# Even mixer of a two-block layer: pooled branch with tokens on partitions, its moving means as a matrix product, low parts on GpSimd, norm pivot from five tiles

## The chip, the cores and the metric

One core of one Trainium2 chip. The metric is device time in microseconds (us) of one execution; the kernel before takes 1034.3 us (median of 3 runs, 1033.93 to 1035.69). Engines: PE is TensorE (PEld its weight load), DVE is VectorE, ACT is ScalarE, POOL is GpSimd, SP issues DMAs.

## The reference, cut to what matters

x is 256 tokens by 1024. A first block (three mixers and a feed-forward) and an odd mixer are not touched. The change is inside the even mixer, whose input product has five parts of 1024 columns:

```python
p = einsum("btd,dn->btn", h, w_in)
a_val, a_glu, a_gate, b_val, b_gate = split(p, ...)
u = causal_depthwise_conv(a_val * sigmoid(a_glu), conv_w, conv_b)   # 31 taps
ya = silu(layernorm(u, ln_g, ln_b)) * silu(a_gate)
d = multiscale_pool_diff(b_val)     # per group of 256 channels: mean of the last w tokens, less b_val; w = 2, 4, 8, 16
d = einsum("btgc,gce->btge", d, pool_w) + pool_b                    # 4 groups of 256 x 256
yb = d * pool_scale * silu(b_gate)
out = concat([ya, yb]) @ w_out      # 2048 -> 1024
```

The mean at token t divides by min(t + 1, w).

## The kernel before, in words

**Products.** Each f32 operand is split into a high part (rounded, fp32r) and a low part (the rest), and a product is three matmuls (`mm3`, L493 to L496). Weights come as a stream of 128x1024 chunks: SP loads `raw` (L315), `split_to` (L329) makes `whi` on ACT (L347) and `wlo` (L350) on POOL or DVE. The first letter of a plan entry names the engine of the high part, the second that of the low part. In the even mixer the plan is `"ag"` (low parts on POOL), but the chunks numbered 11, 13, 15, 18 and 21 of the stage have theirs on DVE (`EVEN_LO_V`, L341). There are four buffers each for high and low parts, and chunks are split two ahead.

**The stage.** h is kept with channels on partitions (`hh`, `hl`, eight 128x256 tiles each). Two of the eight u tiles come from `x_group_m` (h stationary, 512 columns wide). Then `EVEN_ORDER` (L154) runs: u tiles 2 and 3 (two chunks each), eight b chunks, u tiles 4 to 7, eight a (`a_gate`) chunks, eight g (`b_gate`) chunks. Each chunk is one `w_tile` (L498): 24 matmuls of 128x256, which leave an output tile with channels on partitions and tokens along the row. Four PSUM banks named `mm` hold these outputs.

**Side work.** `tick` (L369) advances a queue of generators between matmuls. `conv31(k)` (L1506) makes convolution tile k: ACT makes ten of the 31 taps (L1523) and two starting values (L1513, L1514), DVE adds 19 taps (L1527) and the ACT pieces (L1530) in PSUM; ACT copies one half out (L1533) and DVE adds the other (L1534). POOL then sums the tiles into `csum` (L1541, L1543). `ln_early` (L1552) forms a pivot for the layer norm: a matmul with ones over the sum of tiles 0 to 6 (L1555), scaled by ACT into SBUF (L1558), taken from each tile by DVE (L1547), squared on ACT (L1549) and summed on POOL (L1562, L1564). `ln` (L1567) starts after six ticks of the output product: ones matmuls over the sum and tile 7 (L1571, L1572), then the tail of the norm.

**Pooled branch.** ACT copies each b tile to `bv` (L1646). `pools(g)` (L1618) makes moving sums for group g by 1 to 4 doubling additions on POOL (L1626, L1627), then DVE scales and subtracts (L1634 to L1637). After the last g chunk a loop of eight (L1672) does two f32 matmuls with `pool_w` (L1676), the gate on DVE (L1679) and the split into `yT` (ACT L488, DVE L489).

**Output.** Sixteen chunks (L1684): the pooled half first (k 0 to 7), then the convolved half, whose k = 8 needs `ln` done.

The order of the instructions on each engine is made by the tile scheduler from this program, and each engine runs its list in order.

Of the kernel before, what the change touches and what calls it, by code (L numbers as in the profile page):

```python
# [83 lines left out]
def pack_weights(i):  # L84
# [69 lines left out]
EVEN_ORDER = ([("u", 2), ("u", 3)] + [("b", t) for t in range(8)] + [("u", t) for t in range(4, 8)]  # L154
# [65 lines left out]
CON = {}  # L220


def _con_layout():
    o = 0
    for n, w in (("id", 128), ("tri", 128), ("bo", 128), ("va", 32), ("vm", 32), ("rc", 64), ("cm", 128)):
# [8 lines left out]
def consts():  # L234
# [44 lines left out]
POOL_FROM = 9  # L279


def body(tc, x, wst, vec, gains, rows, con, cmpw, poolw, rgw, igw, out, dbg=None):
# [3 lines left out]
    with ExitStack() as ctx:  # L286
# [42 lines left out]
        def split_to(c):  # L329
            while st["split"] <= min(c, nch - 1):  # L330
# [10 lines left out]
                if plan["p"] is PLAN_EVEN and i - plan.setdefault("i0", i) in EVEN_LO_V:  # L341
                    how = "av"
# [83 lines left out]
        SY.dma_start(cm_t, con[:, CON["cm"][0]:])  # L426
# [1124 lines left out]

        def ln_early():  # L1552

            pps = o_ps()
            PE.matmul(pps[:, 0:T], lhsT=ones, rhs=sums["c"], start=True, stop=True)  # L1555
            lnt = act.tile([P, 512], F32, name="lnt", tag="btok")
            sums["p"], sums["q"] = lnt[:, 0:T], lnt[:, T:2 * T]
            A.activation(sums["p"], pps[:, 0:T], AF.Copy, scale=1.0 / 896)  # L1558
# [8 lines left out]
        def ln():  # L1567
# [3 lines left out]
            PE.matmul(mps[:, 0:T], lhsT=ones, rhs=sums["c"], start=True, stop=False)  # L1571
# [4 lines left out]
            de, va = sums["c"], sums["q"]  # L1576
            V.scalar_tensor_tensor(de, mps[:, 0:T], 1.0 / D, sums["p"], op0=OP.mult, op1=OP.subtract)
# [40 lines left out]
        def pools(g):  # L1618
            n = g + 1
            src = bv[:, 2 * g:2 * g + 2]  # L1620
            cur = src
            w = 2 ** n
            for lv in range(n):
                sh = 2 ** lv
                nx = g4()[:, 0:544].rearrange("p (k t) -> p k t", k=2)
                G.memset(nx[:, :, 0:16], 0.0)  # L1626
                G.tensor_tensor(nx[:, :, 16:], cur[:, :, 16:], cur[:, :, 16 - sh:272 - sh], op=OP.add)  # L1627
                cur = nx
                yield
            d = src[:, :, 16:]  # L1630
            rc = con_t[:, CON["rc"][0] + 16 * g:CON["rc"][0] + 16 * g + 16]
            hd = s(32, "hd")
            hv = hd.rearrange("p (k t) -> p k t", k=2)
            V.tensor_tensor(hv, cur[:, :, 16:32], rc[:, None, :].to_broadcast([P, 2, 16]), op=OP.mult)  # L1634
            V.tensor_tensor(hv, hv, d[:, :, 0:16], op=OP.subtract)
            V.scalar_tensor_tensor(d[:, :, 16:], cur[:, :, 32:], 1.0 / w, d[:, :, 16:], op0=OP.mult, op1=OP.subtract)
            V.tensor_copy(d[:, :, 0:16], hv)  # L1637
            yield

        pools_q = deque()  # L1640
        turn = 0
        for kind, t in EVEN_ORDER:
            ps = mm_ps(T)
            w_tile(ps, hh, hl)
            if kind == "b":
                A.activation(bv[:, t, 16:], ps, AF.Copy)  # L1646
                if t % 2:
                    pools_q.append(pools(t // 2))
            elif kind == "u":
# [6 lines left out]
                if t == 7:  # L1656
# [10 lines left out]
        for pg in pools_q:
            for _ in pg:
                pass
        eh = [yt(), yt()]  # L1670
        el = [yt(), yt()]
        for e in range(8):  # L1672
            g = e // 2
            ps = mm_ps(T)
            for k in range(2):
                PE.matmul(ps, lhsT=pwt[:, g * 512 + k * 256 + (e % 2) * P:g * 512 + k * 256 + (e % 2) * P + P],  # L1676
                          rhs=bv[:, 2 * g + k, 16:], start=k == 0, stop=k == 1)
            d = bg[:, e]
# [193 lines left out]
```

## Time and profile before

| | |
|---|---|
| median of 3 runs | 1034.3 us (1033.93 to 1035.69) |
| the profiled execution | 1034.19 us; span of its records 1032.4 us |
| busy: PE, DVE, ACT, POOL | 971.4, 813.3, 637.8, 281.8 us |
| even mixer, from the first `w_tile` to the first output matmul | 704.6 to 842.8 us of the span |

A row of a group names line, engine, operation and tiles (out<-in), then busy us and mean ns. Of a wait, the row says who waited for whom. The granted clock (PEclk) is 1 at 2.4 GHz and 0.5 at 1.2 GHz. Instructions on one engine overlap a little, so the pace is the distance between starts, not the duration of one.

### The profile page before, as it was taken

The numbers are of one execution on the slowest core, as the hardware profiler recorded it, in microseconds if no ns is written. First come the engines' busy times: TensorE is split into PE (matmuls) and PEld (weight loads), VectorE is DVE, ScalarE is ACT, GpSimd is POOL, SyncE is SP. The second block draws the span as 40 slices with busy tenths as digits, with TensorE's granted clock in tenths as the row PEclk, the third lists the DMA queues.
The fourth block names the chain that finished last, engine by engine and source line by source line (L and its number), as shares of the span: only waits on it lengthen the run. The fifth ranks groups of instructions, "written<-read, shape, count | busy, mean of one in ns | idle before, by whom it ended". The sixth has DMA issues, their size and how long they took to land.

```text
span 1032.4 us, 16952 instructions
## 1 busy us (share of the span) xinstructions
PE 971.4 (94%) x6134; PEld 847.3 (82%) x6134; DVE 813.3 (79%) x1637; ACT 637.8 (62%) x1180; POOL 281.8 (27%) x210
## 2 busy tenths in 40 slices
PE   8999999999999889999999999999899789899786
PEld 5878988788776689888789999989899777799675
DVE  6787999989768599856665555676998989888985
ACT  7453588866665556644555454558757647678563
POOL 1133023310225454200000000007757931334340
PEclk9999999999999999999999999999989999999898
DMA  7756232264544544666756565674444634554432
GB/s 278 227 185 171 91 116 83 90 177 143 163 125 147 177 144 150 201 188 208 232 179 189 183 187 187 190 254 146 122 162 143 184 100 143 186 163 124 143 103 81
DMA packets 48867, 166.94 MB, mean 162 GB/s; under 512 B 5584, under 2 KB 8080, under 8 KB 48528
## 3 DMA queue, kind: packets, MB, share of 16 engines
q1 hardware_dynamic: 45936, 157.21, 48.3%
q10 hardware_dynamic: 1728, 6.55, 1.8%
q0 software_dynamic: 1120, 2.10, 1.0%
q8 instruction: 48, 0.79, 0.3%
q14 instruction: 35, 0.29, 0.1%
HBM read 163.71 MB, written 1.61 MB: 160 GB/s over the span
## 4 chain that ended last, share of the span: by engine, by line
PE 60%; DVE 21%; ACT 6%; issue 5%; POOL 4%; DMA 3%; POOLq 0%; SPq 0%; ACTq 0%; DVEq 0%
PE mm L494 15%; PE mm L496 14%; PE mm L495 14%; DVE wlo L350 4%; PE sc L496 3%; PE sc L495 3%; PE sc L494 3%; ACT whi L347 2%; DVE sc L1527 2%; PE tp L950 2%; PE o L1112 2%; POOL g L820 1%; POOL wlo L350 1%; DVE f L1749 1%; DMA g<-acd 1%
## 5 line engine op out<-in xcount | busy, mean ns | idle before, releaser
L347 ACT ACTIVATE whi<-raw 128x1024 fp32r<-128x1024 f32 x261 | 275.1, 1056 | 170.5 <-PE mm L496 82.3
L350 DVE TENSOR_TENSOR wlo<-raw,whi 128x1024 fp32r<-128x1024 f32 x213 | 274.7, 1291 | 122.2 <-ACT whi L347 120.2
L496 PE MATMUL mm<-hh,wlo 128*128 128x256 f32 x800 | 231.8, 291 | 16.5 <-POOL wlo L350 9.5
L494 PE MATMUL mm<-hh,whi 128*128 128x256 f32 x800 | 233.7, 292 | 2.3 <-ACT f L1660 2.3
L350 POOL TENSOR_TENSOR wlo<-raw,whi 128x1024 fp32r<-128x1024 f32 x56 | 140.9, 2533 | 344.8 <-ACT whi L347 289.2
L495 PE MATMUL mm<-hl,whi 128*128 128x256 f32 x800 | 230.8, 289 | 0.0
L496 PEld LDWEIGHTS mm<-hh,wlo 128*128 128x128 f32 x800 | 157.4, 197 | 18.7 <-POOL wlo L350 10.3
L494 PEld LDWEIGHTS mm<-hh,whi 128*128 128x128 f32 x800 | 157.7, 197 | 5.6 <-issue 2.6
L495 PEld LDWEIGHTS mm<-hl,whi 128*128 128x128 f32 x800 | 157.5, 197 | 1.3 <-issue 0.8
L494 PE MATMUL mm<-whi,yT 128*128 128x512 f32 x320 | 128.0, 402 | 2.6 <-ACT f L1533 1.2
L495 PE MATMUL mm<-wlo,yT 128*128 128x512 f32 x320 | 126.1, 394 | 3.8 <-DVE wlo L350 3.8
L496 PE MATMUL mm<-whi,yT 128*128 128x512 f32 x320 | 125.6, 393 | 0.0
L494 PE MATMUL mm<-whi,hh 128*128 128x512 f32 (+2 forms) x240 | 96.4, 402 | 0.7 <-ACT hh L485 0.5
L495 PE MATMUL mm<-wlo,hh 128*128 128x512 f32 (+2 forms) x240 | 93.8, 391 | 0.4 <-DVE wlo L350 0.4
L496 PE MATMUL mm<-whi,hl 128*128 128x512 f32 (+2 forms) x240 | 93.6, 390 | 0.0
L932 POOL TENSOR_TENSOR t<-t,cf 128x256 f32<-128x256 f32 (+1 forms) x48 | 40.5, 846 | 157.5 <-DVE cf L931 52.8
L494 PEld LDWEIGHTS mm<-whi,yT 128*128 128x128 f32 x320 | 60.6, 190 | 16.5 <-DVE f L1817 2.0
L495 PEld LDWEIGHTS mm<-wlo,yT 128*128 128x128 f32 x320 | 60.6, 190 | 15.9 <-DVE wlo L350 4.7
L496 PEld LDWEIGHTS mm<-whi,yT 128*128 128x128 f32 x320 | 60.4, 189 | 12.9
L1527 DVE SCALAR_TENSOR_TENSOR sc<-f,vec_t,sc 128x256 f32<-128x256 f32 x152 | 65.4, 478 | 2.8 <-ACT sc L1514 2.5
L495 PE MATMUL sc<-hl,whi 128*128 128x256 f32 x224 | 63.5, 283 | 0.0
L496 PE MATMUL sc<-hh,wlo 128*128 128x256 f32 x224 | 63.4, 283 | 0.0
(434 smaller groups left out, 1873.7 us busy)
## 6 DMA issues: line engine op xcount, KB each, us to landing
raw<-in_wst SPq DMA_DIRECT2D x286, 512.0 KB, 3.6
g<-acd SPq DMA_DIRECT2D x8, 512.0 KB, 4.4
gain<-in_gains ACTq DMA_DIRECT2D x4, 512.0 KB, 4.4
f<-in_cmpw ACTq DMA_DIRECT2D x1, 1024.0 KB, 6.7
kB<-iqd POOLq DMA_DIRECT2D x4, 256.0 KB, 5.9
f<-acd SPq DMA_DIRECT2D x2, 512.0 KB, 7.0
f<-in_poolw ACTq DMA_DIRECT2D x1, 1024.0 KB, 4.9
f<-in_rgw ACTq DMA_DIRECT2D x1, 768.0 KB, 4.4
```

The lines of the kernel that those rows point to most:

```text
L347: hi = A.activation(h, w, AF.Copy)
L350: lo = (G if how[1] == "g" else V).tensor_tensor(l, w, h.bitcast(F32), op=OP.subtract)
L494: PE.matmul(ps, lhsT=ah, rhs=bh, start=first, stop=False)
L495: PE.matmul(ps, lhsT=ah, rhs=bl, start=False, stop=False)
L496: PE.matmul(ps, lhsT=al, rhs=bh, start=False, stop=last)
L820: G.tensor_tensor(tv, tv, smb[:, None, :].to_broadcast([P, 8, P]), op=OP.add)
L932: G.tensor_tensor(p, p, cf[:, :, None].to_broadcast([P, 2, nk]), op=OP.mult)
L950: PE.transpose(tp[:, c:c + P], p[:, si, kb * P:kb * P + P], ident)
L1112: PE.matmul(O["o"][g * 64:g * 64 + 64, q * 256:q * 256 + 256], lhsT=xt[:, c % nb, vo + g * 64:vo + g * 64 + 64], rhs=O["t", g][:, c], star ...
L1527: V.scalar_tensor_tensor(h, u[:, tap:tap + T], w(tap), h, op0=OP.mult, op1=OP.add)
L1749: V.tensor_tensor_scan(at(xc, k0 + i), A_(i), I_(i), 0.0, op0=OP.mult, op1=OP.add)
```

## The change

1. **b part with tokens on partitions.** The eight b chunks become two `x_group` calls (h stationary, 512 columns): 96 matmuls of 128x512 in place of 192 of 128x256. ACT copies four 128x512 results into `bt`.
2. **Moving means as a matrix.** "mean of the last w, less itself" is a constant 256x256 band matrix per group; its two non-zero pieces (128x144 and 128x128) are loaded once as `pmt` (128x1088, 544 KB on the ACT queue). `pooled(g)`, called after a chunks 1, 3, 5, 7, makes four f32 matmuls and an ACT copy into `dT`. The POOL additions and the four DVE instructions of each group are gone.
3. **Mixing between the g chunks.** `mixed(e)` (two f32 matmuls, DVE gate, split) follows g chunk e + 2; 6 and 7 follow the last.
4. **All low parts of the stage on POOL**: `EVEN_LO_V` is gone.
5. **Pivot from tiles 0 to 4**, formed after convolution tile 5 and kept in PSUM; `csum` has a half for the first five and one for the rest. The norm's first step is an ACT copy and a DVE subtraction.

```diff
-EVEN_ORDER = ([("u", 2), ("u", 3)] + [("b", t) for t in range(8)] + [("u", t) for t in range(4, 8)]
+EVEN_ORDER = ([("u", 2), ("u", 3)] + [("b", t) for t in range(2)] + [("u", t) for t in range(4, 8)]
               + [("a", t) for t in range(8)] + [("g", t) for t in range(8)])
...
+    tt = np.arange(2 * P)
+    pm = []
+    for w in (2, 4, 8, 16):
+        m = ((tt[:, None] <= tt[None, :]) & (tt[:, None] > tt[None, :] - w)) / np.minimum(tt + 1, w)[None, :]
+        m = m - np.eye(2 * P)
+        pm += [m[:P, :144], m[P:, P:]]
+    put("pm", np.concatenate(pm, axis=1))
...
-                if plan["p"] is PLAN_EVEN and i - plan.setdefault("i0", i) in EVEN_LO_V:
-                    how = "av"
...
             elif k == 0:
-                sums["c"] = act.tile([P, 512], F32, name="csum", tag="cbt")[:, 0:T]
+                sums["c"] = act.tile([P, 512], F32, name="csum", tag="cbt")
             elif k == 1:
-                G.tensor_tensor(sums["c"], cva[:, 0], d, op=OP.add)
+                G.tensor_tensor(sums["c"][:, 0:T], cva[:, 0], d, op=OP.add)
             else:
-                G.tensor_tensor(sums["c"], sums["c"], d, op=OP.add)
+                G.tensor_tensor(sums["c"][:, 0:T] if k < PIVOT else sums["c"][:, T:],
+                                sums["c"][:, T:] if k > PIVOT else sums["c"][:, 0:T], d, op=OP.add)
...
+        def ln_pivot():
+
+            pps = tp_ps()
+            PE.matmul(pps[:, 0:T], lhsT=ones, rhs=sums["c"][:, 0:T], start=True, stop=True)
+            sums["p"] = pps[:, T:]
+            A.activation(sums["p"], pps[:, 0:T], AF.Copy, scale=1.0 / (PIVOT * P))
...
-            V.scalar_tensor_tensor(de, mps[:, 0:T], 1.0 / D, sums["p"], op0=OP.mult, op1=OP.subtract)
+            A.activation(de, mps[:, 0:T], AF.Copy, scale=1.0 / D)
+            V.tensor_tensor(de, de, sums["p"], op=OP.subtract)
...
+        pmt = act.tile([P, 4 * PM], F32, name="pmt", tag="yT", bufs=4)
+        A.dma_start(pmt, con[:, CON["pm"][0]:CON["pm"][1]])
+        def pooled(g):
+
+            ps = mm_ps()
+            for j in range(2):
+                for m, (t0, t1) in enumerate(((0, 144), (P, T))):
+                    c = g * PM + m * 144
+                    f = (2 * g + j) * P
+                    PE.matmul(ps[:, j * T + t0:j * T + t1], lhsT=bt[:, m, f:f + P], rhs=pmt[:, c:c + t1 - t0],
+                              start=m == 0, stop=m == 1, skip_group_check=True)
+            A.activation(dT[:, 2 * g:2 * g + 2], ps.rearrange("p (k t) -> p k t", k=2), AF.Copy)
...
+            if kind == "b":
+                ps = x_group(hk, lk, 8, 512)
+                for m in range(2):
+                    A.activation(bt[:, m, t * 512:t * 512 + 512], ps[m], AF.Copy)
+                tick(rate["n"])
+                continue
...
             elif kind == "a":
                 A.activation(ag[:, t], ps, AF.Silu)
+                if t % 2:
+                    pooled(t // 2)
             else:
                 A.activation(bg[:, t], ps, AF.Silu)
+                if t >= 2:
+                    mixed(t - 2)
...
+        for e in (6, 7):
+            mixed(e)
```

How the lists of instructions move, at three places. Lines in rows of the change are those of the changed file, where L350 has become L358, L1527 L1534, L1530 L1537, L489 L497, L1679 L1655, and L1541 and L1543 L1548 and L1550.

POOL, from the stage's first low parts (`wlo`) to the addition of the third convolution tile into `csum`, before:

```order
L350 TENSOR_TENSOR wlo<-raw,whi 128x1024 x9
L1627 TENSOR_TENSOR g_8036<-f_7425 128x2x256
L350 TENSOR_TENSOR wlo<-raw,whi 128x1024 x2
L1626 MEMSET g_8397 128x2x16
L1627 TENSOR_TENSOR g_8309<-f_7425 128x2x256
...
L1627 TENSOR_TENSOR g_8538<-f_7425 128x2x256
L1541 TENSOR_TENSOR csum<-f_7505 128x256
L350 TENSOR_TENSOR wlo<-raw,whi 128x1024 x3
L1543 TENSOR_TENSOR csum<-csum,f_7505 128x256
```

and now:

```order
L358 TENSOR_TENSOR wlo<-raw,whi 128x1024 x15
L1548 TENSOR_TENSOR csum<-f_7504 128x256
L358 TENSOR_TENSOR wlo<-raw,whi 128x1024 x6
L1550 TENSOR_TENSOR csum<-csum,f_7504 128x256
L358 TENSOR_TENSOR wlo<-raw,whi 128x1024 x4
```

The moving sums are gone from between the low parts, and the first addition into `csum` stands behind 15 low parts, where it stood behind 12.

PE, around the pivot's matmul with ones, before (in g chunk 5) and now (in a chunk 6, after the third `pooled`):

```order
L494 MATMUL mm<-hh,whi 128x256
L495 MATMUL mm<-hl,whi 128x256
L496 MATMUL mm<-hh,wlo 128x256
L1555 MATMUL o<-csum,ones 128x256
L494 MATMUL mm<-hh,whi 128x256
```

```order
L1643 MATMUL mm<-pmt,f_7425 128x144
L1643 MATMUL mm<-pmt,f_7425 128x128
L502 MATMUL mm<-hh,whi 128x256
L503 MATMUL mm<-hl,whi 128x256
L504 MATMUL mm<-hh,wlo 128x256
L502 MATMUL mm<-hh,whi 128x256
L1563 MATMUL tp<-csum,ones 128x256
```

It comes seven chunks earlier, and needs the sum of five tiles instead of seven.

DVE, at the first gate of the pooled branch, now (before, the eight of them, L1679, stand together behind the last g chunk):

```order
L1534 SCALAR_TENSOR_TENSOR sc<-f_7423,vec_t,sc 128x256 x4
L1537 TENSOR_TENSOR sc<-sc,t_8857 128x512
L1534 SCALAR_TENSOR_TENSOR sc<-f_7423,vec_t,sc 128x256
L1655 SCALAR_TENSOR_TENSOR f_7508<-mm,vec_t,f_7508 128x256
L1537 TENSOR_TENSOR sc<-sc,t_8608 128x512
L497 SCALAR_TENSOR_TENSOR yT<-f_7508,vec_t,yT 128x256
```

Gate and low part of `yT` now lie among the taps of convolution tiles 6 and 7, in the time of the g chunks.

## Rows read from the trace of the kernel before

**Rows 1.** Windows of the even mixer: length, busy us (and count) per engine, granted clock, DMA.

```profile
core 0: us, PE busy (x) PEld busy (x) DVE busy (x) ACT busy (x) POOL busy (x), PEclk, DMA share, GB/s
704.60:727.60 23.00, 23.00 (x193) 22.94 (x192) 19.12 (x40) 22.63 (x48) 22.43 (x11) 1.00 0.65 206
727.60:750.00 22.40, 18.30 (x142) 18.09 (x142) 22.40 (x37) 14.93 (x30) 15.30 (x10) 0.90 0.39 117
750.00:784.00 34.00, 29.34 (x210) 28.94 (x209) 28.84 (x57) 21.51 (x40) 16.95 (x9) 0.86 0.45 157
784.00:826.00 42.00, 36.12 (x287) 35.71 (x285) 41.93 (x84) 27.61 (x53) 37.89 (x29) 0.96 0.53 163
826.00:842.80 16.80, 13.81 (x79) 11.50 (x79) 16.31 (x31) 8.12 (x18) 8.11 (x8) 1.00 0.33 94
```

**Rows 2.** PE's waits from 700 to 900 us: us in total, times, longest.

```profile
PE mm L496 <- POOL wlo L350: 9.2, 3, 4.1
PE o L1555 <- POOL csum L1543: 3.2, 1, 3.2
...
PE mm L494 <- ACT f L1660: 2.3, 1, 2.3
PE mm L1676 <- DVE f L1679: 1.3, 2, 0.7
```

**Rows 3.** Timeline of PE: start us, us, what, idle before.

```profile
694.75 0.39 PE L494 MATMUL mm<-whi,hh 128*128 128x512 f32 x1
...
697.25 0.39 PE L496 MATMUL mm<-whi,hl 128*128 128x512 f32 x1
697.48 1.03 PE L627 MATMUL sc<-con_t,t 128*128 128x128 f32 x8
...
707.75 0.28 PE L494 MATMUL mm<-hh,whi 128*128 128x256 f32 x1
...
710.62 0.28 PE L494 MATMUL mm<-hh,whi 128*128 128x256 f32 x1
...
767.10 0.41 PE L494 MATMUL mm<-hh,whi 128*128 128x256 f32 x1
767.31 0.41 PE L495 MATMUL mm<-hl,whi 128*128 128x256 f32 x1
```

**Rows 4.** The pooled mixer's matmuls in that timeline.

```profile
831.47 2.75 PE L1676 MATMUL mm<-f,f 128*128 128x256 f32 x12
```

**Rows 5.** Groups by line, 703 to 860 us: busy us, mean ns, idle before.

```profile
L1636 DVE SCALAR_TENSOR_TENSOR f<-g,f 128x480 f32<-128x480 f32 x4 | 7.7, 1923 | 0.0
L1627 POOL TENSOR_TENSOR g<-g 128x512 f32<-128x512 f32 x6 | 7.4, 1227 | 0.1
L1634 DVE TENSOR_TENSOR hd<-g,con_t 128x32 f32<-128x32 f32 x4 | 6.4, 1595 | 0.0
...
L1547 DVE TENSOR_TENSOR f<-f,lnt 128x256 f32<-128x256 f32 x8 | 5.7, 769 | 1.2 <-PE o L1572 0.8 <-ACT lnt L1558 0.4
...
L1635 DVE TENSOR_TENSOR hd<-hd,f 128x32 f32<-128x32 f32 x4 | 3.6, 892 | 0.0
```

**Rows 6.** Low parts on DVE, 700 to 845 us: ns min/median/max.

```profile
L350 DVE TENSOR_TENSOR wlo<-raw,whi x7: 1214/1654/2967, 730.9 to 844.8; 128x1024 fp32r<-128x1024 f32 x7
```

**Rows 7.** Low parts on POOL, 700 to 845 us: ns min/median/max.

```profile
L350 POOL TENSOR_TENSOR wlo<-raw,whi x33: 2349/2408/3352, 701.9 to 825.8; 128x1024 fp32r<-128x1024 f32 x33
```

**Rows 8.** Timeline of POOL.

```profile
743.23 0.72 POOL L1541 TENSOR_TENSOR csum<-f 128x256 f32<-128x256 f32 x1 [5.96 <-DVE f L1534]
...
800.83 14.15 POOL L350 TENSOR_TENSOR wlo<-raw,whi 128x1024 fp32r<-128x1024 f32 x6
```

**Rows 9.** Timeline of DVE.

```profile
802.93 0.31 DVE L1635 TENSOR_TENSOR hd<-hd,f 128x32 f32<-128x32 f32 x1
...
810.99 1.67 DVE L1634 TENSOR_TENSOR hd<-g,con_t 128x32 f32<-128x32 f32 x1
...
837.42 0.48 DVE L489 SCALAR_TENSOR_TENSOR yT<-f,vec_t,yT 128x256 fp32r<-128x256 f32 x1
```

More of the change, by code (lines that the diff above doesn't have):

```diff
@@ L220 @@
 CON = {}
+PM = 144 + P
 def _con_layout():
     o = 0
[L225 removed]
+    for n, w in (("id", 128), ("tri", 128), ("bo", 128), ("va", 32), ("vm", 32), ("cm", 128), ("pm", 4 * PM)):
         CON[n] = (o, o + w)
@@ L1550, in ln_square @@
             return q
-        def ln_early():
[L1554 to L1558, printed above, removed]
+        def ln_pivot():
[3 more added lines that the diff above has]
+            A.activation(sums["p"], pps[:, 0:T], AF.Copy, scale=1.0 / (PIVOT * P))
+            sums["q"] = act.tile([P, 512], F32, name="lnt", tag="btok")[:, 0:T]
+            yield
+        def ln_early():
             for k in range(7):
@@ L1570, in ln @@
             mps = o_ps()
-            PE.matmul(mps[:, 0:T], lhsT=ones, rhs=sums["c"], start=True, stop=False)
+            PE.matmul(mps[:, 0:T], lhsT=ones, rhs=sums["c"][:, T:], start=True, stop=False)
             PE.matmul(mps[:, 0:T], lhsT=ones, rhs=cva[:, 7], start=False, stop=True)
@@ L1617, in body @@
         side.extend([conv31(0), conv31(1)])
[L1618 to L1638, printed above, removed]
@@ new lines, in mixed @@
+        def mixed(e):
+            g = e // 2
+            ps = mm_ps(T)
+            for k in range(2):
+                PE.matmul(ps, lhsT=pwt[:, g * 512 + k * 256 + (e % 2) * P:g * 512 + k * 256 + (e % 2) * P + P],
+                          rhs=dT[:, 2 * g + k], start=k == 0, stop=k == 1)
+            d = bg[:, e]
+            V.scalar_tensor_tensor(d, ps, vv("pb", e), d, op0=OP.add, op1=OP.mult)
+            split_act(d, yt_[1][0][:, e], yt_[1][1][:, e], scale=vv("psc", e))
+        for kind, t in EVEN_ORDER:
+            if kind == "b":
+                ps = x_group(hk, lk, 8, 512)
+                for m in range(2):
+                    A.activation(bt[:, m, t * 512:t * 512 + 512], ps[m], AF.Copy)
+                tick(rate["n"])
+                continue
@@ L1643, in body @@
             ps = mm_ps(T)
             w_tile(ps, hh, hl)
[L1645 to L1649, printed above, removed]
+            if kind == "u":
                 tick(rate["n"])
@@ L1660, in body @@
                 A.activation(ag[:, t], ps, AF.Silu)
+                if t % 2:
+                    pooled(t // 2)
             else:
                 A.activation(bg[:, t], ps, AF.Silu)
-            turn += 1
-            if pools_q and turn > POOL_FROM and next(pools_q[0], pools_q) is pools_q:
-                pools_q.popleft()
+                if t >= 2:
+                    mixed(t - 2)
             tick(rate["n"])
[L1667 to L1678, printed above, removed]
-            V.scalar_tensor_tensor(d, ps, vv("pb", e), d, op0=OP.add, op1=OP.mult)
-            split_act(d, eh[1][:, e], el[1][:, e], scale=vv("psc", e))
+        for e in (6, 7):
+            mixed(e)
+        yt_[0] = (yt(), yt())
+        eh, el = [[yt_[i][j] for i in range(2)] for j in range(2)]
         side.append(ln())
```

23 lines of the change are left out of this document (11 added, 12 removed).

## The prediction

> **What bounds the kernel now.** I read the windows first, then TensorE's waits, then the timelines of the engines it waits for. The windows [rows 1] show the even mixer from its first 128x256 chunk at 704.6 to its first output matmul at 842.8, 138.2 us. The reader is to see two things in them. TensorE has gaps in every window but the first, and its granted clock falls under 1 there (0.90, 0.86, 0.96). And VectorE is busy 22.40 of 22.40 us and 41.93 of 42.00 in two of the windows where TensorE has its gaps: 19.12 + 22.40 + 28.84 + 41.93 + 16.31 = 128.6 of 138.2.
>
> The waits [rows 2] say for whom TensorE stops: three times for a low part on GpSimd (9.2 us), once for GpSimd's sum of the convolution tiles (3.2), once for a ScalarE activation (2.3), and for the gates of the pooled mixer (1.3). They are 16.0 us. GpSimd is not itself the cause: at 743.23 it had idled 5.96 us for VectorE's end of a convolution tile, and the low part that TensorE needed stood behind that addition [rows 8]. So VectorE is late, GpSimd waits for it in order, and TensorE waits for GpSimd.
>
> TensorE's own work is counted by pace. A chunk of 24 matmuls of 256 columns takes 710.62 - 707.75 = 2.87 us; of 512 columns, eleven starts lie in 697.25 - 694.75 = 2.50 us, 0.227 each [rows 3]. The mixer's 16 f32 matmuls are two records each: twelve records in 2.75 us with the last one lasting about 0.4, so 0.215 a record and 6.9 us for 32 [rows 4]. 36 chunks of 2.87 are 103.3; with the mixer and 0.9 for the pivot and two transposes, 111. The remaining 138.2 - 111 - 16 = 11 us is mostly slow clock: after a stop the starts lie 0.21 apart where they were 0.12 [rows 3], the lower of the two levels (1.2 and 2.4 GHz). The windows give 22.4 x 0.10 + 34 x 0.14 + 42 x 0.04 = 8.7 us for it [rows 1], 1.7 for each of five stops.
>
> **The change, part by part.**
>
> *TensorE.* Eight b chunks (8 x 2.87 = 23.0) become 96 matmuls of 512 columns (96 x 0.227 = 21.8): 1.2 less. The pooled means add 16 f32 matmuls, 32 records of 136 columns on average. No row shows them. Lower bound: f32 records of 128 columns, eight in 1.03 us, the last lasting 0.27, so 0.11 each [rows 3], 3.5 in all. Upper bound: the mixer's 256-column record, 0.215, 6.9 in all [rows 4]. I take 3.7, by columns, near the row of 128. The mixer's 6.9 is moved, not removed. Sum: 28 x 2.87 + 21.8 + 3.7 + 6.9 + 0.9 = 113.7 us, if nothing waits: 24.5 less than 138.2.
>
> *VectorE.* Out go the moving means' instructions (7.7 + 6.4 + 3.6 = 17.7, and four small copies) [rows 5] and five low parts at the median 1.65, 8.3 [rows 6]. The pivot's eight subtractions, 0.77 each beside GpSimd's sums [rows 5], now read the pivot from PSUM. No row shows that form: it costs at most the 0.77 and at least nothing; I price it at the 0.48 of the 256-column step of VectorE that ran while GpSimd idled [rows 9], 2.3 less. Left: 128.6 - 28.3 = 100.3, plus some 2 for the last gates and splits, which before ran after 842.8. That is 102 in 114 us: no longer full, but not loose.
>
> *GpSimd.* Ten additions of up to 1.2 go [rows 5], five low parts of 2.41 come [rows 7]: 12 against 12. Its busy time stays 22.43 + 15.30 + 16.95 + 37.89 + 8.11 = 100.7 [rows 1], now in 114 us. A chunk costs it 2.41 and TensorE 2.87, so it keeps ahead if nothing else stands in its list.
>
> *ScalarE.* 94.8 us now [rows 1]. Eight copies go and eight of twice the width come; one more stands in the norm. It has room, and I cost this at nothing; if its cover went, a high part would come late, a few tenths each.
>
> *DMA.* `pmt` brings 544 KB once over the ACT queue, about one more weight chunk in a stage whose DMA share is 0.33 to 0.65 [rows 1]: nothing. `con_t` is 64 columns narrower at the start: nothing.
>
> *The new waits.* GpSimd's first addition into the sum now stands behind 15 low parts. These end at 701.9 + 15 x 2.41 = 738.1 [rows 7]. It needs convolution tile 1, in the trace ready at 743.2 [rows 8]; ahead of it VectorE loses one L1634 (1.6), one L1636 (1.9) [rows 5] and one low part (1.65) [rows 6], so it comes at about 738. The sixteenth chunk starts on TensorE at 704.6 + 7 x 2.87 + 21.8 = 746.5, so its low part may begin as late as 744.1. That leaves 6 us where TensorE waited up to 4.1 before. The pivot needs five tiles and stands behind the third group of pooled matmuls; I find it within a microsecond of its operands, and charge it to the stops below.
>
> *The tail.* After the last g chunk the eight gates are done but for two, so the output product follows at once. Late next are the end of convolution tile 7, which TensorE's ones matmul needs after three output chunks (36 x 0.227 = 8.2 us later), and the norm, needed at k = 8. Both were hidden before; when the stage shortens by 24 us the VectorE list ahead of them does not shorten by quite as much.
>
> **Sum.** 24.5 less, given back two stops: one at the change of activation functions, whose cause (2.3 us [rows 2]) is untouched, and one of the same size in the tail. Each with its slow clock is 2.3 + 1.7 = 4.0. So 24.5 - 8.0 = 16.5 us. The profiled execution took 1034.19 us (span 1032.4), 0.1 from the median of 1034.3, so 1034.2 - 16.5 = 1017.7: I say **1018 us**.
>
> **The rivals.**
>
> *A. VectorE is held by GpSimd in the g chunks (1022 to 1033, centre 1026).* Low parts on GpSimd run back to back, six in 14.15 us from 800.83 [rows 8]. In that time a VectorE addition of 32 columns took 0.31 us at 802.93 and another of its size 1.67 at 810.99; both end where a low part ends (800.83 + 2.36 = 803.19, + 5 x 2.36 = 812.6) [rows 8, 9]. So a VectorE instruction that reads two SBUF tiles stands still for the rest of GpSimd's. The change moves eight such steps, the low parts of `yT`, from a stretch where GpSimd idled (0.48 us each [rows 9]) into one where it is full. Each can lose from 0 to a whole low part, 2.41 [rows 7]: 0 to 19 us. Half is 9.6; with VectorE some 6 us ahead of need, that makes a stop of 4 plus the slow clock at the ones matmul and at k = 8, so 1018 + 8 = 1026; at the upper end 1033. For it: the shortened stage leaves VectorE only 12 us. Against: the steps are spread, and TensorE's chunk is longer than a low part, so GpSimd has gaps.
>
> The Trainium skill, SBUF — State Buffer, section "Who interferes with whom", says that a VectorE instruction with two SBUF inputs contends with a GpSimd instruction that reads SBUF, and that the loser blocks for the whole instruction. By that rule alone each of the eight would lose 1.2 us on average and the five low parts sent to GpSimd speak against the change; the two rows agree with it.
>
> *B. GpSimd's list becomes the brake (1046, slower).* All low parts now stand in one list with the six additions into the sum; before, five could pass on VectorE. If VectorE ends each convolution tile over 6 us later than I reckon, each addition holds the next low part as at 743.23, and TensorE stops 4.1 [rows 2] plus 1.7 of slow clock, 5.8 each. 24.5 / 5.8 = 4.2, so from the fifth of six on the kernel is slower; at six, 1034.2 - 24.5 + 34.8 = 1044.5, with a late pivot about 1046. For it: that is the mechanism in the trace. Against: VectorE loses 28 us of work ahead of these additions.
>
> *C. The change does not move the end (1033 to 1035).* Convolution tile 7 and the norm end no sooner, since VectorE fills what was freed with waiting for its operands; TensorE then stops before k = 8 for what it saved. It would take 24 us of new VectorE idling; there were some 10 in 138.
>
> *D. Nothing stops (1009.7).* 1034.2 - 24.5. Against it: the stop at the change of activation functions is untouched [rows 2].
>
> **How the numbers follow.** The forecast, 1011 to 1022 (none to three stops, pooled matmuls at either bound), 0.58; A 0.27; B 0.05; C 0.05; D 0.05. The range that leaves out 2 in 10 is 1010 to 1029: it drops C, B, the upper third of A and a little of D. A measurement here can tell some 0.2%, 2 us, from no change. Faster by more: 0.58 + 0.27 + 0.05 and a fifth of C, 0.91; within it 0.04; slower 0.05.
>
> **What would show it.** Right: the stage from first chunk to first output matmul is 114 to 124 us; the waits for POOL low parts fall from 9.2 us to under 3; the granted clock is at 1.00 in most of its windows; VectorE shows idle time there. A: the low parts of `yT` take over 1 us on VectorE, and TensorE waits for the ones matmul after three output chunks or before k = 8. B: waits for POOL `wlo` over 9 us, each behind a `csum` addition. C: a shorter stage and a wait of the same size in the output product. The pooled matmuls are mispriced if 32 records take over 7 us. The forecast is wrong as a whole if the even mixer keeps its 138 us or if time moves outside it, since nothing else in the program changes but a few instructions that the scheduler swaps.

## The result, and the profile after

The changed kernel takes 1011.7 us (median of 4 runs, 1011.49 to 1012.3), the kernel before 1034.6 beside it: a ratio of 0.978, 95% interval 0.976 to 0.980. The forecast was 1018 in a range of 1010 to 1029: the direction and the stage were right, the time 6 us too long, and the result lies 1.7 us above the lower end of the range.

Windows of the changed kernel's even mixer, columns as in [rows 1]; the last one begins at the first output matmul:

```profile
704.60:727.60 23.00, 23.00 (x144) 20.83 (x144) 19.20 (x41) 22.82 (x47) 22.14 (x10) 1.00 0.70 220
727.60:750.00 22.40, 22.40 (x152) 20.80 (x151) 20.58 (x48) 18.93 (x36) 19.90 (x9) 1.00 0.63 195
750.00:784.00 34.00, 34.00 (x283) 33.79 (x282) 29.25 (x68) 30.51 (x61) 28.92 (x15) 1.00 0.56 171
784.00:817.40 33.40, 33.40 (x254) 32.19 (x252) 29.52 (x63) 21.91 (x44) 25.00 (x16) 1.00 0.48 143
817.40:842.80 25.40, 23.99 (x103) 18.94 (x103) 23.11 (x41) 15.18 (x24) 3.38 (x4) 1.00 0.52 166
```

TensorE has no gap from the first chunk (703.31) to the first output matmul (817.41): 114.1 us where [rows 1] had 138.2, and the granted clock is 1.00 in every window. VectorE, full in two windows of [rows 1], now has idle time in each.

TensorE's waits, 695 to 880 us (us in total, times, longest), the counterpart of [rows 2]:

```profile
PE sc L635 <- DVE t L619: 2.3, 1, 2.3
PE mm L502 <- DVE f L1655: 1.4, 2, 1.2
PE mm L503 <- DVE walt L358: 0.8, 1, 0.8
PE mm L502 <- ACT whi L355: 0.5, 1, 0.5
...
```

No low part, no sum and no activation is waited for inside the stage. The 1.4 us lie behind it: the first output matmuls wait for the last gates, which in [rows 2] held the pooled matmuls inside the stage (1.3 us).

Timeline of the changed kernel (POOL, PE, ACT and DVE rows, in order of time), the counterpart of [rows 8, 9]:

```profile
738.50 0.74 POOL L1548 TENSOR_TENSOR csum<-f 128x256 f32<-128x256 f32 x1 [0.54 <-DVE f L1541]
764.28 1.28 ACT L1680 ACT_TABLE_LOAD   x1
786.41 1.10 PE L1643 MATMUL mm<-pmt,f 128*128 128x144 f32 x8
799.76 2.66 DVE L497 SCALAR_TENSOR_TENSOR yT<-f,vec_t,yT 128x256 fp32r<-128x256 f32 x1 [1.62 <-ACT yT L496]
799.76 4.91 POOL L358 TENSOR_TENSOR wlo<-raw,whi 128x1024 fp32r<-128x1024 f32 x2
812.72 1.04 DVE L497 SCALAR_TENSOR_TENSOR yT<-f,vec_t,yT 128x256 fp32r<-128x256 f32 x1
819.55 0.50 PE L502 MATMUL mm<-whi,yT 128*128 128x512 f32 x1 [1.18 <-DVE f L1655]
821.51 0.50 PE L502 MATMUL mm<-whi,yT 128*128 128x512 f32 x1 [0.23 <-DVE f L1655]
```

GpSimd idled 0.54 us before its first addition into the sum, where [rows 8] has 5.96.

Groups of the changed kernel, 703 to 845 us, the counterpart of [rows 5, 7]:

```profile
L497 DVE SCALAR_TENSOR_TENSOR yT<-f,vec_t,yT 128x256 fp32r<-128x256 f32 x8 | 6.6, 820 | 1.6 <-ACT yT L496 1.6
L1555 DVE TENSOR_TENSOR f<-f,tp 128x256 f32<-128x256 f32 x8 | 3.3, 417 | 2.1 <-PE o L1584 1.2 <-ACT tp L1565 0.6 <-POOL csum L1550 0.2
L358 POOL TENSOR_TENSOR wlo<-raw,whi 128x1024 fp32r<-128x1024 f32 x37 | 88.8, 2419 | 11.0 <-ACT whi L355 10.4
```

The difference of the two spans is the sum of three stretches. The stage is 138.17 - 114.10 = 24.07 us shorter. It begins 704.59 - 703.31 = 1.28 earlier; in the profiles of this study it begins anywhere from 702.0 to 707.5, and next to nothing ahead of it is changed. From the first output matmul to the end it is 192.39 against 189.64, 2.75 longer. 24.07 + 1.28 - 2.75 = 22.6 = 1032.4 - 1009.8.

The lengthening lies right behind the stage. Timelines of TensorE, before (two rows) and after (two rows): the first output matmul, and the ones matmul over convolution tile 7.

```profile
842.76 0.47 PE L494 MATMUL mm<-whi,yT 128*128 128x512 f32 x1 [1.24 <-ACT f L1533]
851.03 0.59 PE L1572 MATMUL o<-f,ones 128*128 128x256 f32 x2
...
817.41 0.50 PE L502 MATMUL mm<-whi,yT 128*128 128x512 f32 x1
828.24 0.59 PE L1584 MATMUL o<-f,ones 128*128 128x256 f32 x2
```

The distance was 851.03 - 842.76 = 8.27 us and is 828.24 - 817.41 = 10.83, so 2.56 of the 2.75 us arise there: 0.43 from a ones matmul that before lay inside the stage, the rest around the stops for the last gates.

### The profile page after: what moved, and what is told of

Same layout as the page of the kernel before. It is cut to its first block, busy times and chain, and to the rows that moved or that the text cites. A ratio compares the mean times of both kernels' runs of the same rounds, so it can differ in the third digit from the quotient of the medians.

```text
span 1009.8 us, 16786 instructions
## 1 busy us (share of the span) xinstructions
PE 967.3 (96%) x6070; PEld 839.3 (83%) x6070; DVE 785.2 (78%) x1616; ACT 639.1 (63%) x1181; POOL 280.0 (28%) x194
## 4 chain that ended last, share of the span: by engine, by line
PE 63%; DVE 20%; ACT 6%; DMA 5%; issue 4%; POOL 2%; SPq 0%; POOLq 0%; DVEq 0%; ACTq 0%
PE mm L502 16%; PE mm L503 15%; PE mm L504 15%; DVE wlo L358 4%; PE sc L504 3%; PE sc L503 3%; PE sc L502 3%; ACT whi L355 2%; DMA raw<-in_wst 2%; PE tp L958 1%; PE o L1120 1%; POOL g L828 1%; DVE f L1760 1%; DMA f<-acd 1%; DMA g<-acd 1%
## 5 line engine op out<-in xcount | busy, mean ns | idle before, releaser
L358 DVE TENSOR_TENSOR wlo<-raw,whi 128x1024 fp32r<-128x1024 f32 x208 | 264.6, 1274 | 120.6 <-ACT whi L355 120.0
L358 POOL TENSOR_TENSOR wlo<-raw,whi 128x1024 fp32r<-128x1024 f32 x61 | 151.5, 2497 | 346.9 <-ACT whi L355 291.6
L504 PE MATMUL mm<-hh,wlo 128*128 128x256 f32 x736 | 211.0, 287 | 7.0 <-DVE wlo L358 6.7
L502 PE MATMUL mm<-hh,whi 128*128 128x256 f32 x736 | 213.6, 290 | 0.0
L503 PE MATMUL mm<-hl,whi 128*128 128x256 f32 x736 | 210.3, 286 | 0.0
L504 PEld LDWEIGHTS mm<-hh,wlo 128*128 128x128 f32 x736 | 142.2, 193 | 8.6 <-DVE wlo L358 7.1
L502 PEld LDWEIGHTS mm<-hh,whi 128*128 128x128 f32 x736 | 142.2, 193 | 3.5 <-issue 2.7
L503 PEld LDWEIGHTS mm<-hl,whi 128*128 128x128 f32 x736 | 142.2, 193 | 1.4 <-issue 0.8
L502 PE MATMUL mm<-whi,hh 128*128 128x512 f32 (+2 forms) x272 | 108.3, 398 | 1.2 <-ACT whi L355 0.8
L503 PE MATMUL mm<-wlo,hh 128*128 128x512 f32 (+2 forms) x272 | 105.7, 389 | 0.8 <-DVE wlo L358 0.4
L504 PE MATMUL mm<-whi,hl 128*128 128x512 f32 (+2 forms) x272 | 105.8, 389 | 0.0
L1534 DVE SCALAR_TENSOR_TENSOR sc<-f,vec_t,sc 128x256 f32<-128x256 f32 x152 | 66.1, 483 | 4.4 <-ACT sc L1521 3.6
```

The lines of the kernel that those rows point to most:

```text
L358: lo = (G if how[1] == "g" else V).tensor_tensor(l, w, h.bitcast(F32), op=OP.subtract)
L502: PE.matmul(ps, lhsT=ah, rhs=bh, start=first, stop=False)
L503: PE.matmul(ps, lhsT=ah, rhs=bl, start=False, stop=False)
L504: PE.matmul(ps, lhsT=al, rhs=bh, start=False, stop=last)
L1534: V.scalar_tensor_tensor(h, u[:, tap:tap + T], w(tap), h, op0=OP.mult, op1=OP.add)
```

## The experiments

Theory V: VectorE is late with the convolution tiles, GpSimd waits for it in order, TensorE for GpSimd, so the gain comes from VectorE's 28 us. Rivals: the gain comes from the low parts (L), from the early pivot (P), or from GpSimd's own list (G). The table holds all runs; "stage" is from the first 128x256 matmul to the first output matmul of the profiled run, and the three columns behind it are of that stretch.

| kernel | median us | stage | VectorE busy | TensorE waits | clock |
|---|---|---|---|---|---|
| before | 1034.6 | 138.2 | 128.6 | 16.4 | 0.94 |
| pivot alone | 1034.0 | 138.9 | 122.7 | 17.0 | 0.93 |
| low parts alone | 1020.1 | 124.0 | 114.2 | 7.9 | 0.99 |
| low parts alone, VectorE's load put back | 1031.2 | 134.9 | 125.7 | 14.9 | 0.94 |
| before, sum on VectorE | 1028.7 | 130.1 | 122.9 | 12.1 | 0.96 |
| pooled branch alone | 1024.2 | 126.8 | 109.3 | 8.4 | 0.97 |
| low parts and pivot | 1022.4 | 125.1 | 110.1 | 9.8 | 0.99 |
| change without the low parts | 1020.1 | 123.6 | 106.6 | 6.5 | 0.97 |
| change without the pivot | 1014.1 | 116.9 | 101.7 | 1.9 | 1.00 |
| the change | 1011.7 | 114.1 | 99.0 | 0 | 1.00 |
| mixing in a block | 1012.1 | 117.1 | 100.0 | 1.3 | 1.00 |
| mixing one chunk earlier | 1008.3 | 113.8 | 99.1 | 0 | 1.00 |
| change, no pooled matmuls | 1014.6 | 113.7 | 96.1 | 2.1 | 0.98 |
| change, 48 more additions on VectorE | 1051.5 | 138.4 | 133.3 | 18.3 | 0.95 |

### Each part alone, on the kernel before

**Low parts alone.**

```diff
-EVEN_LO_V = (11, 13, 15, 18, 21)
...
-                if plan["p"] is PLAN_EVEN and i - plan.setdefault("i0", i) in EVEN_LO_V:
-                    how = "av"
```

> The kernel before with all low parts of the even mixer on GpSimd and nothing else. Theory V: of VectorE's 8.3 us only one low part of 1.65 lies ahead of the first addition into the sum, so GpSimd comes free hardly sooner and has 12 us more to do: 1030 to 1038, waits for GpSimd's low parts as long as before (9.2 us) or longer. Rival L (this move carries the gain): 1022 to 1028. Rival G (GpSimd's list is the brake): clearly slower, 1038 to 1046.

Measured: 1020.1 us, ratio 0.988 (0.985 to 0.991). Theory V's number was missed by 10 us and rival L's surpassed: 14.1 us for an edit that gives GpSimd five low parts more (its busy time in the stage rose from 100.7 to 107.9 us). Its stage as one window, columns as in [rows 1]:

```profile
705.04:829.02 123.98, 114.69 (x903) 112.20 (x902) 114.17 (x234) 94.05 (x186) 107.89 (x68) 0.99 0.57 170
```

VectorE's busy time fell by 128.6 - 114.2 = 14.4 us, and the stage by 14.2. I had counted only the one low part ahead of the first addition.

**Pivot alone.**

```diff
+PIVOT = 5
...
+        def ln_pivot():
...
+                if t == 6:
+                    side.append(ln_pivot())
```

> The kernel before with the pivot from five tiles, kept in PSUM, and nothing else. Theory V: the eight subtractions lose up to 2.3 us and the ones matmul no longer waits 3.2 us for the sum, but VectorE stays full and GpSimd late: 1028 to 1034. Rival P (the pivot carries the gain): 1024 or less. Rivals L and G: no change, 1033 to 1036.

Measured: 1034.0, ratio 1.0005 (0.9987 to 1.0024): nothing. VectorE is 6 us less busy, but TensorE now waits 5.2 us at the pivot's matmul, behind GpSimd. Rival P falls.

**Low parts and pivot.** Both edits together.

> The kernel before with both the low parts on GpSimd and the early pivot: the change without its pooled branch. Theory V: near the sum of the two parts alone, 1026 to 1036, so that the pooled branch is worth over 14 us on top. Rivals L and P: 1022 or less. Rival G: 1036 to 1046, the same as the low parts alone.

Measured: 1022.4, ratio 0.990 (0.986 to 0.993): the low parts' gain and no more, 3.6 us under V's range. The pooled branch is worth 1022.4 - 1011.7 = 10.7 on top.

**Pooled branch alone** (the change, without the two edits above).

> The changed kernel with two of its parts undone: five low parts are back on VectorE, and the pivot is the old one from seven tiles. What is left is the pooled branch alone (matrix product, mixing between the g chunks). Theory V (VectorE was late with the convolution tiles, GpSimd waited for it in order, TensorE for GpSimd; the pooled branch takes 17.7 of the 28.3 us off VectorE): most of the gain is here, 1012 to 1020 us, with VectorE near 112 us busy in a stage of 115 to 122. Rival L (the low parts moved off VectorE carry the gain): 1026 or more. Rival P (the early pivot carries it, by taking away the 3.2 us wait at the ones matmul): the wait at the ones matmul is back, and the time is 1018 or more. Rival G (what counts is the ten additions taken out of GpSimd's list): 1010 to 1012, since GpSimd now has five low parts less besides.

Measured: 1024.2, ratio 0.991 (0.988 to 0.994). V wanted at most 1020, G at most 1012, L at least 1026; P's "1018 or more" holds, but the pivot alone gave nothing. V's range was missed by 4.2 us. VectorE is down to 109.3, but the stage is 17.5 longer than that. Its timeline shows why:

```profile
757.71 0.72 POOL L1553 TENSOR_TENSOR csum<-csum,f 128x256 f32<-128x256 f32 x1 [8.72 <-DVE f L1544]
761.77 0.58 PE L507 MATMUL mm<-hh,wlo 128*128 128x256 f32 x1 [3.83 <-POOL wlo L361]
767.28 1.06 ACT L358 ACTIVATE whi<-raw 128x1024 fp32r<-128x1024 f32 x1 [4.64 <-PE mm L506]
773.31 1.28 ACT L1675 ACT_TABLE_LOAD   x1
```

GpSimd, with less to do, stood 8.72 us before its second addition; the low part that TensorE needed came behind it, TensorE stopped, and ScalarE stood for TensorE. More idle time on GpSimd did not help: rival G falls.

### Each part taken out of the change

**Without the low parts' move** (the three lines above put back).

> The changed kernel with five low parts back on VectorE. Theory V: VectorE has 8.3 us more in a stage where it was some 10 to 15 us short of full, so it comes later where TensorE waits for it: 1012 to 1018, waits for VectorE or for the sum return. Rival L: 1020 or more. Rival G (GpSimd's list sets the stage): faster or the same, 1009 to 1012, since GpSimd loses 12 us.

Measured: 1020.1, ratio 0.986 (0.984 to 0.988), so the move is worth 8.4 us here. The same 8.7 us wait of GpSimd and 3.8 of TensorE as with the pooled branch alone are back. V's range reached 1018; L's "1020 or more" is met.

```profile
755.55 0.42 DVE L1544 TENSOR_TENSOR f<-f,sc 128x256 f32<-128x256 f32 x1 [2.49 <-ACT f L1543]
```

VectorE was not full here: it idled 2.49 us before it ended the third convolution tile, 2.8 us later than in the changed kernel (752.78). What differs more is GpSimd's list. The second addition into the sum stands behind 15 low parts (13 ahead of the first addition, 2 more behind it), in the changed kernel behind 21 (15 and 6), so GpSimd came to it early and stood there. By these rows a full VectorE is not the whole of it: where the additions stand in GpSimd's list counts too.

**With the old pivot.**

> The changed kernel with the old pivot (from seven tiles, kept in SBUF). Theory V: VectorE's subtractions cost some 2.5 us more, and the ones matmul stands at g chunk 5 again and needs tile 6: a wait of 0 to 4 us with its slow clock, 1012 to 1018. Rival P: 1018 or more. Rivals L and G: 1011 to 1012, no difference.

Measured: 1014.1 (1012.43 to 1019.14), ratio 0.981 (0.978 to 0.983): 2.3 us slower in the median, but the interval overlaps that of the change. The profiled run was the slowest of the four, so its 1.9 us wait at the ones matmul and its stage of 116.9 us, which fit V, are not those of the median run.

### VectorE's load put back, and the ring cut

After these runs two readings of the 14 us were left: VectorE's time (V), or the place of the additions in GpSimd's list (R). In the trace of the kernel before, its timeline read across the engines shows a ring of waits:

```profile
747.29 0.58 PE L496 MATMUL mm<-hh,wlo 128*128 128x256 f32 x1 [4.10 <-POOL wlo L350]
752.83 0.39 ACT L1654 ACTIVATE sq<-mm 128x256 f32<-128x256 f32 x1 [7.22 <-PE mm L496]
761.64 0.42 DVE L1534 TENSOR_TENSOR f<-f,sc 128x256 f32<-128x256 f32 x1 [2.24 <-ACT f L1533]
762.20 0.74 POOL L1543 TENSOR_TENSOR csum<-csum,f 128x256 f32<-128x256 f32 x1 [5.56 <-DVE f L1534]
766.29 0.58 PE L496 MATMUL mm<-hh,wlo 128*128 128x256 f32 x1 [2.36 <-POOL wlo L350]
770.73 1.06 ACT L347 ACTIVATE whi<-raw 128x1024 fp32r<-128x1024 f32 x1 [4.37 <-PE mm L495]
777.13 1.28 ACT L1660 ACT_TABLE_LOAD   x1
778.86 0.39 PE L494 MATMUL mm<-hh,whi 128*128 128x256 f32 x1 [2.30 <-ACT f L1660]
```

TensorE's stop holds ScalarE, ScalarE's late piece holds VectorE's next tile, VectorE's late tile holds GpSimd's next addition, and GpSimd's late low part stops TensorE again: one lap per convolution tile, 19 us from the first stop to the second.

**The five subtractions made on VectorE as well**, with all low parts on GpSimd as in the low parts alone:

```diff
...
+                        V.tensor_tensor(plan["scr"][:, 0:CH], w, h.bitcast(F32), op=OP.subtract)
...
```

> The kernel before with all low parts on GpSimd, which alone took 1020.1 us, and in addition the five old subtractions still made on VectorE, into a tile that nothing reads. GpSimd's list is that of the run at 1020, VectorE's load that of the kernel before or a little more. Theory V (what the moved low parts gave was VectorE's time): the gain is gone, 1030 to 1037. Theory R with the place in GpSimd's list as the cause (with more low parts in its list, each addition into the sum stands behind low parts that TensorE needs sooner): most of the gain stays, 1020 to 1025.

Measured: 1031.2, ratio 0.996 (0.995 to 0.997). 11.1 of the 14.1 us are gone again. What was put back, one line's instructions on DVE (ns min/median/max):

```profile
L354 DVE TENSOR_TENSOR f<-raw,whi x5: 1210/1923/2897, 730.7 to 774.5; 128x1024 f32<-128x1024 f32 x5
```

Their sum is 10.1 us (five of 2.02 in the mean), about as much as the time that came back. Some 3 us remain for the other reading (3.9 against the kernel before, 1035.1 beside it).

GpSimd's list is not quite that of the low parts alone, as the expectation has it. The six additions keep their place: they stand behind 16, 21, 26, 31, 36 and 38 low parts, with the low parts alone behind 15, 20, 26, 30, 35 and 38, in the kernel before behind 12, 15, 19, 23, 29 and 32. But the scheduler put part of the moving sums behind the third addition again, as in the kernel before. Nor did the load take VectorE's time only: GpSimd's busy time rose from 107.9 to 113.1 us, and the dummy subtractions held the buffers of raw weights, for which the loads and then ScalarE waited:

```profile
SPq L315 <- DVE f L354: 9.6, 4, 3.9
ACT whi L349 <- DMA raw<-in_wst: 5.0, 2, 2.8
```

So the run shows that the gain goes when these steps are put back on VectorE while the additions keep their place; how much of it is VectorE's own time, and how much these effects, it does not separate.

**The additions into the sum on VectorE**, low parts as before:

```diff
-                G.tensor_tensor(sums["c"], cva[:, 0], d, op=OP.add)
+                V.tensor_tensor(sums["c"], cva[:, 0], d, op=OP.add)
...
-                G.tensor_tensor(sums["c"], sums["c"], d, op=OP.add)
+                V.tensor_tensor(sums["c"], sums["c"], d, op=OP.add)
```

> The kernel before with the six additions into the sum of the convolution tiles moved from GpSimd to VectorE; the five low parts stay on VectorE. Theory R (a ring of waits: TensorE stops for a low part that stands behind an addition on GpSimd; its stop holds ScalarE, which holds VectorE's next tile, which holds GpSimd's next addition): the ring is cut although VectorE gets some 2.5 us more (six times 0.41), so the three waits for GpSimd's low parts (9.2 us) with their slow clock go, 1018 to 1027 us. Theory V alone (VectorE's load in the stage sets its length): VectorE has more to do, 1035 to 1038.

Measured: 1028.7, ratio 0.994 (0.992 to 0.997), 6.4 us less, 1.7 above the upper end of R's range. GpSimd's list no longer holds what waits for a convolution tile, and of the 9.2 us of waits for its low parts 0.2 are left, although VectorE has six additions more. In their place TensorE waits 6.0 us for the sum at the ones matmul (3.2 before) and 3.2 for two low parts on VectorE. The run does not separate the ring from VectorE's load, since VectorE was 5.7 us less busy in the stage, for all the six additions (122.9 against 128.6). Both readings stand: putting VectorE's load back takes most of the low parts' gain away, and the place of the additions makes GpSimd's low parts late; that the ring multiplies the load is read from the trace and not shown by a run. TensorE's waits, and VectorE's own low parts:

```profile
PE o L1555 <- DVE csum L1543: 6.0, 1, 6.0
PE mm L496 <- DVE wlo L350: 3.2, 2, 1.9
PE mm L496 <- POOL wlo L350: 0.2, 1, 0.2
...
L350 DVE TENSOR_TENSOR wlo<-raw,whi x6: 1214/1216/1467, 733.9 to 826.5; 128x1024 fp32r<-128x1024 f32 x6
```

They took 1.22 us where [rows 6] has a median of 1.65 and up to 2.97. During the two from 751.42 and 760.74 GpSimd ran nothing at all.

**48 more additions on VectorE in the changed kernel.**

```diff
+            for _ in range(3):
+                V.tensor_tensor(scr, bt[:, 0, 0:256], bt[:, 1, 0:256], op=OP.add)
...
+            if (kind, t) in DUM:
+                dummy()
```

> The changed kernel with 48 additions of 128x256 that nothing uses on VectorE, three after each of sixteen chunks of the stage; the output is the same. In the trace of the changed kernel such an addition of two SBUF tiles took about 0.4 us with GpSimd idle, so they give VectorE back some 19 of the 28 us that the change took off it, or more where GpSimd holds them. Theory V: VectorE is full again, the additions into the sum come late, GpSimd's low parts stand behind them: 1020 to 1035, with waits for GpSimd's low parts of several us and a granted clock under 1. Rival G (GpSimd's ten additions were the cause): 1012 to 1016, VectorE's load does not reach TensorE.

Measured: 1051.5, ratio 1.016 (1.011 to 1.021), beyond V's range, with the clock at 0.95 in the stage and waits of 18.3 us. The dose was mispriced:

```profile
L1663 DVE TENSOR_TENSOR scr<-f x48: 406/514/2658, 728.9 to 838.3; 128x256 f32<-128x256 f32 x48
```

At a mean of 1.03 us they were 49.2 us, not 19, and the time rose by 39.8; in the profile 24.3 of that lie in the stage and 12.4 behind it. From 728.9 to 838.3 VectorE was full (109.0 of 109.4 us). G, which wanted 1016 at most, is excluded. But V's path is not the one taken: no wait in the stage is for a low part on GpSimd. The longest are these:

```profile
PE tp L1563 <- POOL csum L1550: 7.1, 1, 7.1
PE mm L502 <- ACT f L1691: 5.0, 1, 5.0
```

VectorE's load reaches TensorE by the pivot's sum and by ScalarE as well.

### What bounds the changed kernel

**Without the sixteen pooled matmuls.**

```diff
...
-                    PE.matmul(ps[:, j * T + t0:j * T + t1], lhsT=bt[:, m, f:f + P], rhs=pmt[:, c:c + t1 - t0],
-                              start=m == 0, stop=m == 1, skip_group_check=True)
-            A.activation(dT[:, 2 * g:2 * g + 2], ps.rearrange("p (k t) -> p k t", k=2), AF.Copy)
+            A.activation(dT[:, 2 * g:2 * g + 2], bt[:, g // 2, g % 2 * 512:g % 2 * 512 + 512].rearrange("p (k t) -> p k t", k=2), AF.Copy)
```

> The changed kernel without the sixteen matmuls of the moving means: the tile that they fill is filled by a copy of the b part, so the means of the last w tokens are left out. It prices them where nothing waits. If TensorE is now the bound of the stage: 3.5 to 4.0 us less than the changed kernel (32 records of 0.117), 1007.5 to 1008.5. If VectorE or GpSimd bounds it still: under 1.5 us less, 1010.2 or more.

Measured: 1014.6 (1010.67 to 1015.41), ratio 0.981 (0.979 to 0.983): no gain at all; the median is 3 us higher, with overlapping intervals. This kernel leaves out the moving means. Its timeline:

```profile
782.45 0.70 PE L1563 MATMUL tp<-csum,ones 128*128 128x256 f32 x2 [2.11 <-POOL csum L1550]
794.98 0.42 DVE L1541 TENSOR_TENSOR f<-f,sc 128x256 f32<-128x256 f32 x1 [4.89 <-ACT f L1540]
832.41 0.37 ACT L1540 ACTIVATE f<-sc 128x256 f32<-128x256 f32 x1
849.98 0.80 PE L502 MATMUL mm<-whi,yT 128*128 128x512 f32 x1 [6.19 <-ACT yT L493]
```

TensorE reached the pivot 2.1 us before its sum, and k = 8 of the output 6.2 us before the norm: the copy of the last convolution tile came at 832.41, in the changed kernel at 824.20. The convolution came later, not as before: VectorE waited 4.89 us for ScalarE's copy at the sixth tile (1.00 in the changed kernel), and the scheduler put six low parts of the output ahead of VectorE's end of the last tile, where the changed kernel has three. So the run shows that 3.75 us less of TensorE's work gave nothing here, and that the sum and the norm are close behind; that TensorE's 114 us and the convolution's end are level is not shown, because the lists moved with the edit.

**Mixing in a block behind the g chunks.**

```diff
-                if t >= 2:
-                    mixed(t - 2)
...
-        for e in (6, 7):
+        for e in range(8):
```

> The changed kernel with the eight mixing products and gates in one block behind the last g chunk, as before, in place of between the g chunks. Theory V: TensorE's work is the same, so what is added is the block's own waits: 1.3 us for the gates [the old wait], and the first output matmuls wait for eight gates on VectorE instead of two: 1013 to 1018. Rival: the interleaving carries little, 1011 to 1013, since VectorE's eight low parts of yT would go back to a stretch where GpSimd idles and lose nothing to it.

Measured: 1012.1, ratio 0.978 (0.977 to 0.979), the same as the change: the rival was right, the interleaving carries nothing that could be measured. The stage is 3.0 longer and what follows it 3.0 shorter; in place of the 1.4 us for the last gates TensorE waits 1.3 for gates inside the stage and 1.3 for the norm at k = 8.

**Mixing one chunk earlier.**

```diff
-                if t >= 2:
-                    mixed(t - 2)
+                if t >= 1:
+                    mixed(t - 1)
...
-        for e in (6, 7):
+        for e in (7,):
```

> The changed kernel with each mixing product one g chunk earlier: only the last of the eight is left behind the last g chunk. In the trace of the changed kernel the first output matmuls wait 1.4 us for the last gates on VectorE. Theory: that wait falls to about half or goes, 1010 to 1011.7. Rival: the gate now comes before its Silu is done or holds VectorE sooner, and TensorE waits within the g chunks for what it saved: 1011.5 to 1013.

Measured: 1008.3 (1007.95 to 1011.67), ratio 0.975 (0.974 to 0.977), 1.7 us under the theory's range. The 1.4 us wait for the gates is gone, and from the first output matmul to the end it takes 190.5 us instead of 192.4. It is the fastest version of the study. Of its 3.4 us to the changed kernel, 1.3 lie ahead of the stage, where the two programs are alike, and the two intervals overlap: about 2 us are explained, the rest is not.

## Why the prediction was right, and by what it missed

**What bounds the kernel: right, but half of the chain.** Theory V held: in the runs with VectorE at 114 us or more, all but the pivot alone, the stage is 5 to 10 us longer than VectorE's busy time, and a load put back on it returned 0.8 to 1.1 times its own time. Not all of the waits came that way. With the low parts put back into the change VectorE was 106.6 us busy in a stage of 123.6, and GpSimd stood 8.7 us before an addition that stands earlier in its list. What the prediction did not see is that this place counts, and that TensorE's stop can also make VectorE late, as the ring above is read.

**TensorE's sum: right.** 113.7 us if nothing waits; measured 114.1, and nothing waited. That is the lower end of the 114 to 124 us that were to show the forecast right. The pooled records, bounded by 3.5 and 6.9 and taken at 3.7: eight in 1.10 us with the last one 0.28, so (1.10 - 0.28) / 7 = 0.117 each, 3.75 for 32.

**VectorE's sum: near.** 102 predicted, 99.0 measured. The pivot's subtraction from PSUM, taken at 0.48, took 0.417 [rows 5 have 0.769 for the old form]. The five low parts were priced at the median of 1.65 of [rows 6], 8.3 in all; the stage's low parts on VectorE fell from 11.0 us (six) to 1.4 (one) when they moved, 9.6. The rest of the 14.4 is the balance of other steps: L1634 went from 6.4 to 3.2 us and the pivot's subtractions from 5.3 to 2.6, L1635 up from 3.6 to 5.4.

**GpSimd: right.** The first addition came at 738.5, predicted about 738. Busy 97.3, predicted 100.7.

**The stops: wrong, and this is 5.3 of the 6.1 us.** The step that failed is "given back two stops: one at the change of activation functions, whose cause (2.3 us [rows 2]) is untouched, and one of the same size in the tail", 8.0 us. The first did not occur. The stop is there (1.6 to 2.3 us, right at the table load) in the five kernels of the table that keep low parts on VectorE, and in none of the nine that have them all on GpSimd: the change did touch its cause. In four of the five ScalarE had stood over 4 us for TensorE some 6 us earlier (4.37 at 770.73 in the kernel before), so the table load of 1.28 us came late, at 777.13; in the changed kernel it came at 764.28 and nobody waited. With the sum on VectorE the stop came without such a hold, so the ring is not all of its cause; what else it is stays open. The second was 1.4 us (1.18 + 0.23), and the clock stayed at 1.00 around it. Charged were 8.0; measured is 2.75 of lengthening behind the stage, those 1.4 among it, so 5.25 us less. From 1017.7 to the profiled 1011.6 are 6.1 us: another 1.28 is the earlier start of the stage, which the change does not explain and which is luck, and 0.43 goes the other way, by which the stage was longer than its sum.

**Rival A: its mechanism was there, its price was not.** The eight low parts of `yT` took 6.6 us where eight of 0.48 are 3.8; two were held (2.66 and 1.04), six were not. The two began while a GpSimd instruction ran, the six while GpSimd stood idle. The 2.8 us lie in a stretch where GpSimd was busy 25.0 of 33.4 us, and TensorE waited for none of them there. Half of the full price, 9.6, was too much: three of the eight came only behind the stage, and GpSimd's waits, mostly for ScalarE (10.4 us in the stage), leave gaps for others.

**Rivals B, C and D.** B: GpSimd waited 0.5 + 0.9 us before its additions, not 4 each. C did not occur in the change, but it is what stopped the run without pooled matmuls at k = 8: the forecast was right to name the norm as late next. D, at 1009.7, was nearest and had been given 0.05 because of the stop at the change of activation functions. The forecast's band begins at 1011 with "none" of the stops, but its own sum gives D's 1009.7 there.

**The parts.** Alone they give 10.0 (pooled), 14.1 (low parts) and 0.2 (pivot); taken out of the whole they cost 10.7, 8.4 and 2.3. The prediction took the pooled branch for the larger share (17.7 against 8.3 us of VectorE); the runs have it the other way round for the parts alone, and the prediction's way round, with 10.7 against 8.4, for the parts taken out. Alone, the pooled branch left GpSimd 14.0 us of waits before its additions (2.3 + 11.7), the low parts 0.5.

## What to carry to other kernels

When several engines that run in order wait for each other in turn, a stop makes the next one: follow one stop around all engines before pricing any, and when its cause goes, do not keep charging a stop because its own instruction is unchanged. Take work off the engine that is full in the window, and price it at what it costs beside its neighbour, not alone. Once the waits are gone, look for the bound that is level with the new one: here 3.75 us less of TensorE work gave nothing, because the convolution's end and the norm came no sooner, but later. And when a scheduler makes the lists, compare them before saying that an edit changed one thing only.

## What the runs showed of the hardware

The same VectorE subtraction of 128x1024 from SBUF took 1.22 us in one kernel, twice with GpSimd idle, and up to 2.97 in another, where GpSimd's low parts ran beside it, and 48 additions of 128x256 took from 0.41 to 2.66 us, 1.03 in the mean and 0.51 in the median. So a price taken from a few rows can be wrong by more than a factor of two either way: the 48 additions were priced at 19 us and took 49.2, the loss of the eight low parts of `yT` at 9.6 and was 2.8. The loss is mutual: in the kernel before two low parts on GpSimd took 6.64 us (from 743.91), against 2 x 2.41, while VectorE ran two of its own.

The Trainium skill, SBUF — State Buffer, section "Who interferes with whom", says that a VectorE instruction with two SBUF inputs contends with a GpSimd instruction that reads SBUF, and that the port pair they share is an exclusive lock. The rows agree with that: 2.66 is within one GpSimd low part (2.41) and the step's own 0.48. How often a step is held depends on whether GpSimd runs when it begins: here two of eight were held, the two that began while GpSimd ran, and the median of the 48 is only 0.1 above their shortest.
